# A seven-product scheme for the Fourier columns of an encoder's input projection

## The chip, the cores and the metric

The kernel runs on one core of a Trainium2 chip. The metric is device time in microseconds (us) of one execution of the whole program. A core has five engines with a queue each: TensorE (PE, matrix products, with its weight loads shown apart as PEld), VectorE (DVE), ScalarE (ACT), GpSimd (POOL) and SyncE (SP, which here only starts DMA transfers). DMA transfers are started from the queues of SP, ACT and POOL.

## What is computed

The reference is one encoder layer on 768 positions (512 of one request, 256 of another), width 2048, in float32:

```python
h = rmsnorm(x, ln_mix_g)
z = h @ w_in                       # 2048 x 2560: 1024 Fourier columns, then q 1024, k 256, v 256
of = fourier_mix(zf, w_fourier)    # Re(2-D DFT over positions and a group's 128 channels), then a 128x128 map, 8 groups
q, k = apply_rope(q), apply_rope(k)
oa = window_attention(q, k, v, attn_sink)     # 16 q heads, 4 kv heads, +-128 positions
x = x + concat(rmsnorm(of), rmsnorm(oa)) @ w_out
u = relu(rmsnorm(x, ln_mlp_g) @ w_up)
x = x + (u * u) @ w_down           # D_FF = 8192
```

and a final RMSNorm. The change is inside `z = h @ w_in`, for the Fourier columns, and in what follows it up to the attention.

## The kernel before

**Number format.** Each float32 operand of a large product is split into a high part, rounded to the multiplier's format by an ACT copy, and a low part, the DVE's difference (`split`, line 66). A product is then three matmuls: high x high, high x low, low x high. Every matmul has a 128x128 weight operand and a moving operand of up to 512 columns, and adds into one of eight PSUM banks.

**Stages.** (1) Lines 205 to 335: x is loaded in six blocks `m` of 128 rows, transposed on PE (`four`), scaled by the gains and split (`evacuate`) into `hh` and `hl`, four tiles of [128, 4, 768] each, which stay on the chip. The v columns are multiplied in the same stage (`v_proj`, line 221). The factor of the RMS norm is not applied to h: it is kept per position, and as a row `rb` (`row_scale`, line 242). (2) Lines 338 to 622: the other 2304 columns, in 36 **pieces**. A pair of 128 columns each takes four pieces, one per 512 rows of `w_in`; a piece is 512 KB of weights and 48 matmuls of 384 columns (2 column blocks x 4 k-blocks x 3 terms x 2 halves of the positions, line 602). `piece_load` and `piece_split` (lines 567, 575) fetch and split the weights, one piece ahead of the products, through two buffers `raw` and four each of `wh` and `wl`. At the end of a pair the DVE multiplies the sums by `rb` (line 615) and ACT's queue writes them to DRAM: `zf_d` (Fourier), `zk_d` (keys), `zq_d` (queries). The order of the columns is Fourier (16 pieces), k (4), q (16). (3) Attention and the output projection, interleaved. (4) The two MLP products, each already a scheme of seven products of half size.

**What runs beside the pieces.** A table `todo` (lines 540 to 560) hangs work on the middle (k + 0.5 is popped in the middle of piece k + 1) or the end of a piece. Each Fourier group has `load_group` (its z back from DRAM), `fold` (line 357, folding by symmetry on the DVE, and 4 small matmuls), `stage1` (three calls) and `stage2` (line 420, the DFT products; then ACT and DVE copy the result out, POOL squares it and adds it to `ssf`, lines 434 to 438). A group starts every second piece. `fourier_norm` (line 442) sums `ssf` with twelve one-column matmuls, one piece after the last `stage2`. Then `open_attention` loads the rotary tables, and 16 **jobs** (`keys`, `queries`, lines 485 and 495) each load half a 128-row block of k or q and its rows swapped by 32 (five DMAs, `rows2`, line 473), rotate it (one POOL and two DVE instructions, line 463), split it, and write queries back. `load_q`, `split_q` (lines 508, 529) prepare the first attention units, and `load_of` and `out_split` the first blocks of the output projection.

**What sets the order.** PE's instructions run in the order of the program text. ACT, DVE and SP do so only inside the `manual_schedule` blocks; elsewhere a scheduler at build time orders each queue. On the chip each queue runs in order: an instruction that waits holds all behind it on its engine. A tile with `bufs=n` waits until the use n allocations ago has ended.

Of the kernel before, what the change touches and what calls it, by code (L numbers as in the profile page):

```python
# [20 lines left out]
P = 128  # L21
# [4 lines left out]
NM = T // P  # L26
# [14 lines left out]
def hybrid_encoder(ctx: ExitStack, tc: tile.TileContext, a: dict):  # L41
# [74 lines left out]
    zk_d = [dpool.tile([P, T], F32, tag=f"zk{i}", name=f"zk{i}") for i in range(2)]  # L116
    zq_d = [dpool.tile([2 * P, T], F32, tag=f"zq{i}", name=f"zq{i}") for i in range(NKV)]
# [4 lines left out]
    x1_d = [[dpool.tile([P, 512], F32, tag=f"x1_{m}_{n}", name=f"x1_{m}_{n}") for n in range(4)] for m in range(NM)]  # L122

# [71 lines left out]
    with ExitStack() as ph:  # L195
        hp = ph.enter_context(tc.tile_pool(name="hp", bufs=1, reuse_waits="tile"))
        zp = ph.enter_context(tc.tile_pool(name="zp", bufs=2, reuse_waits="tile"))
        pp = ph.enter_context(tc.tile_pool(name="pp1", bufs=6, space=PSUM))
        hh, hl = [], []
        for j in range(4):  # L200
            hh.append(hp.tile([P, 4, T], F32R, tag=f"hh{j}", name=f"hh{j}"))
            hl.append(hp.tile([P, 4, T], F32R, tag=f"hl{j}", name=f"hl{j}"))
        rb = hp.tile([P, T], F32, tag="rb", name="rb")

        with tc.tile_pool(name="xp", bufs=2, reuse_waits="tile") as xp:

# [14 lines left out]
            def v_proj(m, between=None):  # L221

                pv = pp.tile([P, 512], F32, tag="ps", name="pv")
                t0 = slice(m * P, (m + 1) * P)
                high = [(hh, 0, j) for j in range(4)]
                low = [(hl, 0, j) for j in range(4)], [(hh, 1, j) for j in range(4)]
                if between is not None:
                    seq = [x for pair in zip(high, low[0]) for x in pair] + low[1]
                else:
                    seq = high + low[1] + low[0]  # L230
                for n, (l, r, j) in enumerate(seq):
                    if n == 10 and between is not None:
                        between()
                    for i in range(4):
                        nc.tensor.matmul(  # L235
                            pv[:, :256], l[j][:, i, t0], wv[j][r][:, i, :],
                            start=(n == 0 and i == 0), stop=(n == 11 and i == 3),
                        )
# [3 lines left out]
            def row_scale(m):  # L242
# [5 lines left out]
                pb = pp.tile([P, 512], F32, tag="f", name="pb", bufs=2)  # L248
# [3 lines left out]
            def load_wv(j):  # L252
                raw = xp.tile([P, 4, 256], F32, tag="raw", name="raw", bufs=4)
                nc.sync.dma_start(raw[:], w_in[:, 4 * j : 4 * j + 4, IN_W - 256 :])
                return raw
# [10 lines left out]
            def gains(r, n, c0):  # L266

                pg = pp.tile([P, 512], F32, tag="f", name="pg", bufs=2)
# [3 lines left out]
            with tc.manual_schedule(engines={mybir.EngineType.SP}):  # L272
# [3 lines left out]
                wv = [load_wv(j) for j in range(4)]  # L276
# [3 lines left out]
            def four(m):  # L280
                pts = [pp.tile([P, 512], F32, tag="ps", name="pt") for _ in range(4)]
# [6 lines left out]
            def evacuate(m, pts, js, between=lambda: None):  # L288
                ts = slice(m * P, (m + 1) * P)
                tmps = [(j, scale_rows(xp, pts[j], g0[:, 4 * j : 4 * j + 4], 4)) for j in js]  # L290
                between()
                for j, tmp in tmps:
                    nc.scalar.activation(hh[j][:, :, ts], tmp[:], AF.Copy)
                for j, tmp in tmps:
                    nc.vector.tensor_tensor(out=hl[j][:, :, ts], in0=tmp[:], in1=f32(hh[j][:, :, ts]), op=ALU.subtract)
# [4 lines left out]
            def idle(n):  # L300

                pw = pp.tile([P, 512], F32, tag="f", name="pw", bufs=2)
# [4 lines left out]
            with tc.manual_schedule(engines={mybir.EngineType.SP, mybir.EngineType.Activation, mybir.EngineType.DVE}):  # L307
# [8 lines left out]
                for m in range(NM):  # L316
# [12 lines left out]
                    if m + 3 < NM:  # L329
                        xts.append(load_x(m + 3))  # L330
                    if m > 0:
                        v_split = v_proj(m)
                v_split()
                row_scale(NM - 1)

# [4 lines left out]
        nc.sync.dma_start(cc[:], a["c_chan"])  # L340
        tabh = fp.tile([P, 4, 256], F32R, tag="tabh", name="tabh")
        tabl = fp.tile([P, 4, 256], F32R, tag="tabl", name="tabl")
        for i in range(2):
            tab = fp.tile([P, 2, 256], F32, tag="zf", name="tab", bufs=2)
            nc.sync.dma_start(tab[:], a["c_pos"][:, 2 * i : 2 * i + 2, :])
            split(tabh[:, 2 * i : 2 * i + 2, :], tabl[:, 2 * i : 2 * i + 2, :], tab[:])
        ssf = fp.tile([P, T], F32, tag="ssf", name="ssf")
        fst = {}

# [6 lines left out]

        def fold(g):

            z, wf = fst.pop(g)
            pc = pp.tile([P, 512], F32, tag="f", name="pc", bufs=2)  # L360
# [29 lines left out]
        def stage1(g, b):  # L390
            sh, sl, cw, ah, al = fst[g]
            pa = pp.tile([P, 512], F32, tag="f", name="pa", bufs=2)
# [27 lines left out]
        def stage2(g):  # L420
            ah, al = fst.pop(g)[3:]
            pe = pp.tile([P, 512], F32, tag="f", name="pe", bufs=2)
            pz = pp.tile([P, 512], F32, tag="f", name="pz2", bufs=2)
# [18 lines left out]
        def fourier_norm():  # L442
            ps_r = pp.tile([P, 512], F32, tag="f", name="ps_r", bufs=2)
# [8 lines left out]
        def open_attention():  # L452
            kp = kt["kp"] = kctx.enter_context(tc.tile_pool(name="kp", bufs=1, side="right", reuse_waits="tile"))
            for name, shape, src in (
# [4 lines left out]
                nc.sync.dma_start(kt[name][:, : src.shape[1]], src)  # L459
            kt["kdh"] = kp.tile([P, NKV, T], F32R, tag="kdh", name="kdh")  # L460
# [12 lines left out]
        def rows2(src, s):  # L473

            t0 = slice(s * HALF, (s + 1) * HALF)
            x, y = (kt["kp"].tile([P, 1, 512], F32, tag=c, name=c, bufs=n)[:, :, :HALF] for c, n in (("rx", 2), ("ry", 2)))
            z = src[:, t0].rearrange("p (o t) -> p o t", o=1)
            nc.sync.dma_start(x, z)
            for r in range(0, P, 64):
                nc.sync.dma_start(y[r : r + 32], z[r + 32 : r + 64])  # L480
                nc.sync.dma_start(y[r + 32 : r + 64], z[r : r + 32])
            rotate(x, y, t0)
            return x[:, 0, :], t0

# [1114 lines left out]
```

## Time and profile before

| what | value |
|---|---|
| time, median of 3 runs (lowest to highest) | 2608.66 us (2608.39 to 2608.85) |
| the profiled execution's own time | 2609.26 us |
| its span, first to last instruction | 2607.5 us |
| DVE, ACT, POOL busy | 67%, 41%, 9% of the span |
| DMA | 465.17 MB, mean 178 GB/s |
| granted TensorE clock | 0.999 |

A row of a group of instructions reads: line, engine, operation, output <- inputs by the program's tile names, shapes, xcount, then busy time, mean ns of one instruction, and the idle time of the engine just before them with what ended it. A row of the timeline or of the chain of waits starts with its start and its duration in us. Matmuls overlap in the pipeline, so the mean duration of one is longer than its share of PE's time. A row of the busy-time table gives a stretch of the span, its length, busy us and number of instructions of PE, PEld, DVE, ACT and POOL, the granted clock, the DMA engines' busy share and GB/s.

### The profile page before, as it was taken

How to read it: one execution, taken by the hardware profiler on the slowest of the kernel's cores; microseconds unless marked ns; L12 is line 12 of the kernel's file. 1: busy time of each engine (PE TensorE's matmuls, PEld its weight loads, DVE VectorE, ACT ScalarE, POOL GpSimd, SP SyncE). 2: the span in 40 equal slices, each digit the busy share in tenths (PEclk: the TensorE clock that was granted, in tenths of full speed). 3: DMA queues.
4: the chain of work that ended last, by engine and by line, in shares of the span. 5: the costliest groups of instructions: out<-in, count | busy, mean ns of one | idle time of the engine just before them, and what ended most of it. 6: DMA issues, size and time to landing. Idle time of an engine off the chain costs nothing.

```text
span 2607.5 us, 35144 instructions
## 1 busy us (share of the span) xinstructions
PE 2593.1 (99%) x13676; PEld 2375.5 (91%) x13676; DVE 1745.5 (67%) x2194; ACT 1079.2 (41%) x1551; POOL 247.4 (9%) x347
## 2 busy tenths in 40 slices
PE   9999999999999999999999999999999999999998
PEld 9999998888899999999999999988888888888887
DVE  6334448777655656555777787757776765777687
ACT  6233327775333333333554445433333333333335
POOL 1011212233210011000000000010000000000000
PEclk9999999999999999999999999999999999999999
DMA  5323466345664555466666666685543672554364
GB/s 178 122 95 111 137 219 187 112 126 173 198 225 151 174 169 177 147 204 244 206 213 214 224 234 213 219 325 177 182 159 111 208 249 74 177 185 157 98 209 155
DMA packets 255047, 465.17 MB, mean 178 GB/s; under 512 B 20080, under 2 KB 151712, under 8 KB 254240
## 3 DMA queue, kind: packets, MB, share of 16 engines
q1 hardware_dynamic: 189936, 305.01, 36.2%
q10 hardware_dynamic: 53120, 110.46, 11.1%
q0 software_dynamic: 11824, 47.46, 5.3%
q8 instruction: 107, 1.75, 0.3%
q14 instruction: 60, 0.49, 0.1%
HBM read 344.10 MB, written 118.75 MB: 178 GB/s over the span
## 4 chain that ended last, share of the span: by engine, by line
PE 97%; DVE 2%; DMA 1%; issue 0%; POOL 0%; ACT 0%; SPq 0%; DVEq 0%; POOLq 0%; ACTq 0%
PE pu L980 36%; PE pd L1415 35%; PE pz L602 12%; PE pm L834 9%; PE pv L235 1%; PE s L645 1%; PE o L721 1%; PE t L702 1%; PE pe L427 0%; PE pa L406 0%; PE ptx L134 0%; PE pt L134 0%; DMA raw<-in_w_in 0%; DVE p L660 0%; DVE wl L70 0%
## 5 line engine op out<-in xcount | busy, mean ns | idle before, releaser
L980 PE MATMUL pu<-xf,wh 128*128 128x384 f32 x3072 | 780.1, 334 | 0.0
L980 PEld LDWEIGHTS pu<-xf,wh 128*128 128x128 f32 x3072 | 554.0, 188 | 1.5 <-ACT o L998 1.3
L1415 PE MATMUL pd<-wh,sh 128*128 128x512 f32 x1332 | 517.7, 389 | 0.0
L1415 PE MATMUL pd<-wl,sh 128*128 128x512 f32 x1332 | 517.7, 389 | 0.0
L1415 PE MATMUL pd<-wh,sl 128*128 128x512 f32 x1332 | 517.5, 389 | 0.0
L980 PE MATMUL pu<-xf,wl 128*128 128x384 f32 x1536 | 513.1, 334 | 0.0
L1392 ACT ACTIVATE wh<-rd 128x1024 fp32r<-128x1024 f32 x200 | 202.5, 1055 | 522.0 <-PE pd L1415 424.3
L1402 DVE TENSOR_TENSOR wl<-rd,wh 128x1024 fp32r<-128x1024 f32 x200 | 236.1, 1222 | 226.1 <-ACT wh L1392 225.4
L960 ACT ACTIVATE wh<-ur 128x1024 fp32r<-128x1024 f32 x160 | 170.3, 1064 | 383.6 <-PE pu L980 207.9
L1415 PEld LDWEIGHTS pd<-wh,sl 128*128 128x128 f32 x1332 | 250.0, 188 | 52.1 <-DVE sl L1403 0.3
L1415 PEld LDWEIGHTS pd<-wh,sh 128*128 128x128 f32 x1332 | 250.1, 188 | 51.8
L1415 PEld LDWEIGHTS pd<-wl,sh 128*128 128x128 f32 x1332 | 250.1, 188 | 51.5
L980 PEld LDWEIGHTS pu<-xf,wl 128*128 128x128 f32 x1536 | 288.3, 188 | 0.0
L966 DVE TENSOR_TENSOR wl<-ur,wh 128x1024 fp32r<-128x1024 f32 x160 | 195.6, 1222 | 76.3 <-ACT wh L960 76.3
L1001 DVE TENSOR_TENSOR o<-pu,o 128x768 f32<-128x768 f32 x160 | 152.9, 956 | 121.7 <-PE pu L980 114.2
L602 PE MATMUL pz<-hh,wh 128*128 128x384 f32 x576 | 147.7, 337 | 0.0
L602 PE MATMUL pz<-hh,wl 128*128 128x384 f32 x576 | 146.2, 334 | 0.0
L602 PE MATMUL pz<-hl,wh 128*128 128x384 f32 x576 | 146.2, 334 | 0.0
L1385 DVE TENSOR_TENSOR rd<-rd 128x1024 f32<-128x1024 f32 x112 | 131.8, 1218 | 0.0
L980 PE MATMUL pu<-xs,wh 128*128 128x384 f32 x512 | 129.8, 334 | 0.0
L960 ACT ACTIVATE wh<-sx 128x1024 fp32r<-128x1024 f32 x64 | 67.9, 1063 | 130.0 <-PE pu L980 107.1
L70 DVE TENSOR_TENSOR wl<-raw,wh 128x1024 fp32r<-128x1024 f32 x56 | 68.3, 1226 | 66.5 <-ACT wh L69 64.8
(253 smaller groups left out, 3715.2 us busy)
## 6 DMA issues: line engine op xcount, KB each, us to landing
rd<-in_w_down SPq DMA_DIRECT2D x176, 512.0 KB, 4.9
ur<-in_w_up SPq DMA_DIRECT2D x128, 512.0 KB, 3.9
sr<-sd SPq DMA_DIRECT2D x95, 384.0 KB, 5.1
pd<-o ACTq DMA_DIRECT2D x60, 384.0 KB, 2.3
o<-pd POOLq DMA_DIRECT2D x60, 384.0 KB, 5.8
sd<-sm ACTq DMA_DIRECT2D x60, 384.0 KB, 2.8
raw<-in_w_in SPq DMA_DIRECT2D x40, 512.0 KB, 3.5
raw<-in_w_out SPq DMA_DIRECT2D x32, 512.0 KB, 4.2
```

What stands on the lines that cost most here:

```text
L70: nc.vector.tensor_tensor(out=lo, in0=src, in1=f32(hi), op=ALU.subtract)
L235: nc.tensor.matmul(pv[:, :256], l[j][:, i, t0], wv[j][r][:, i, :], start=(n == 0 and i == 0), stop=(n == 11 and i == 3),)
L602: nc.tensor.matmul(ps[c][s][:, :HALF], w[:, i, cs], h[j][:, i, s * HALF : (s + 1) * HALF], start=first and n == 0, stop=stop and n == 2,)
L834: nc.tensor.matmul(ps, l(k), w[:, k % 2, :], start=(k == 0 and n == 0), stop=(k == 7 and n == 2))
L960: nc.scalar.activation(wh[:], raw[:], AF.Copy)
L966: nc.vector.tensor_tensor(out=wl[:], in0=raw[:], in1=f32(wh[:]), op=ALU.subtract)
L980: nc.tensor.matmul(ps[:, t, :HALF], w[:, i, t * P : (t + 1) * P], xb[:, o, i, :], start=(s == first_of[bank] and i == 0 and n == 0), stop= ...
L1001: nc.vector.tensor_tensor(out=o, in0=src, in1=o, op=ALU.add)
L1385: add = lambda x, y, op: nc.vector.tensor_tensor(out=x[:], in0=x[:], in1=y[:], op=op)
L1392: nc.scalar.activation(wh[:], t[:], AF.Copy)
L1402: nc.vector.tensor_tensor(out=wl[:], in0=t[:], in1=f32(wh[:]), op=ALU.subtract)
L1415: nc.tensor.matmul(o, l[:, q, ts], w[:, ns], start=(j == j0 and (q, t) == (0, 0)), stop=(j == j1 and (q, t) == (1, 2)),)
```

## The change

Each group of 512 Fourier columns is cut in two halves of 256 (weight blocks `a1k`, `a2k`, k the half of the 2048 inner rows), the positions in two halves of 384 (`bk1`, `bk2`). In place of eight half-size products per group there are seven, in the order `a11, s1, s2, s3, a22, s4, a12`, where s1 = a21 + a22, s2 = s1 - a11, s3 = a11 - a21, s4 = a12 - s2, each times its own block or difference of position blocks. The sums of weights are made on the DVE from two loaded blocks; s1 and s2 are written to DRAM from POOL's queue and loaded again where a later sum needs them. The position blocks are kept unsplit (`xr`), and their differences, high and low parts are made during the products, in two buffers `xs`. A product is four pieces n (2 column groups x 2 halves of its inner rows) of 24 matmuls of 384 columns; there are 28 of them. `load7` runs 5 pieces ahead, `sum7` and `high7` 3, `low7` 2. Products share PSUM banks X, Y, Z; partial results are copied out (`out7`), added and written to `zf_d`.

The 20 pieces of k and q follow, with the split two pieces ahead and four `ps` banks in place of six; `f` banks go from two to four. `rb` is applied later: to z in `fold`, and to the rotary tables. The end-of-pair copies go from DVE to ACT. `zk_d` and `zq_d` hold 32 more rows per head, so that the swapped rows are read with one DMA, after two more writes. Fourier groups start every piece instead of every second one, `fourier_norm` stands half a piece after the last `stage2`, and jobs start every half piece. In the x stage, PSUM pools and the order of `v_proj`'s terms change.

The diff, cut to its core:

```diff
-        pp = ph.enter_context(tc.tile_pool(name="pp1", bufs=6, space=PSUM))
...
+        pp = ph.enter_context(tc.tile_pool(name="pp1", bufs=4, space=PSUM))
+        xr = [[hp.tile([P, 8, HALF], F32, tag=f"xr{k}{t}", name=f"xr{k}{t}") for t in range(2)] for k in range(2)]
+        xs = [hp.tile([P, 2, 8, HALF], F32R, tag=f"xs{i}", name=f"xs{i}") for i in range(2)]
...
+        names7 = ("a11", "s1", "s2", "s3", "a22", "s4", "a12")
+        terms7 = {"s1": ("a21", "a22", ALU.add), "s2": ("s1", "a11", ALU.subtract), "s3": ("a11", "a21", ALU.subtract), "s4": ("a12", "s2", ALU.subtract)}
+        bank7 = {"a11": "X", "s1": "Y", "s2": "X", "s3": "X", "a22": "X", "s4": "Y", "a12": "Z"}
...
+        def load7(n):
...
+            for i, x in enumerate(terms7.get(s, (s,))[:2]):
+                if n < 2 or i > 0:
+                    raw = wpool.tile([P, 4, 256], F32, tag="raw", name="raw", bufs=2)
+                else:
+                    raw = hq["p"].tile([P, 4, 256], F32, tag="wr", name="wr", bufs=5)
...
+                nc.vector.tensor_tensor(out=x[:], in0=x[:], in1=y[:], op=terms7[s][2])
+                if s in w1_d:
+                    nc.gpsimd.dma_start(w1_d[s][g][e][:], x[:])
...
+            x = xs[w % 2]
+            for i in range(4):
+                for r in range(2):
+                    for q, (l, o) in enumerate(((wh, 0), (wh, 1), (wl, 0))):
+                        nc.tensor.matmul(
+                            ps7[bank, g, r][:, :HALF], l[:, i, r * P : (r + 1) * P], x[:, o, 4 * e + i, :],
...
+        for e in range(2):
+            step(high_at, e, lambda e=e: xhigh(h1, b11, e))
+            step(low_at, e, lambda e=e: xlow(l1, b11, h1, e))
+            step(low_at, 2 + e, lambda e=e: xsum(b11, b22, b11, e))
+            step(high_at, 4 + e, lambda e=e: xhigh(h0, b11, e))
+            step(low_at, 4 + e, lambda e=e: xlow(l0, b11, h0, e))
+            step(low_at, 7 + 2 * e, lambda e=e: difference(e))
+            step(high_at, 8 + 2 * e, lambda e=e: xhigh(h1, fx["d"], e))
...
+            for n in range(NP7):
+                for fn in high_at.get(n, ()):
+                    fn()
+                sum7(n + 3)
+                high7(n + 3)
+                low7(n + 2)
+                for fn in low_at.get(n, ()):
+                    fn()
+                product7(n)
+                out7(n - 1)
+                load7(n + 5)
...
             z, wf = fst.pop(g)
+            nc.vector.tensor_tensor(out=z[:], in0=z[:], in1=rb[:], op=ALU.mult)
...
-            p0 = 5.5 + 2 * g
+            p0 = (0.5, 1.5, 2.5, 3.5, 4.5, 5.5, 6.5, 7.5)[g]
...
-        after(22.5, fourier_norm)
-        after(23, open_attention)
+        after(10, fourier_norm)
+        after(10, open_attention)
...
+            t = 10.5 + 0.5 * i
+            after(t - 0.5, lambda i=i, src=src, s=s: job_load(i, src, s))
...
-                        nc.vector.tensor_tensor(out=zs[:, hs], in0=ps[c][s][:, :HALF], in1=rb[:, hs], op=ALU.mult)
+                        nc.scalar.copy(zs[:, hs], ps[c][s][:, :HALF])
```

More of the change, by code (lines that the diff above doesn't have):

```diff
@@ L229, in v_proj @@
                 else:
-                    seq = high + low[1] + low[0]
+                    seq = [x for three in zip(high, low[1], low[0]) for x in three]
                 for n, (l, r, j) in enumerate(seq):
@@ L564, in hybrid_encoder @@
+        dst = [zk_d[i][:] for i in range(2)]
+        dst += [zq_d[i // 2][i % 2 * 2 : i % 2 * 2 + 2] for i in range(8)]
+        cols = [2048, 1024, 1280, 1536, 1792]
         n_in = 4 * len(cols)
```

307 lines of the change are left out of this document (227 added, 80 removed).

## The prediction

> **What bounds the kernel now.** I read the page first (engines, then the chain that ended last), then the busy time of the stage that changes, then the chain inside it.
>
> ```profile
> PE 2593.1 (99%) x13676; PEld 2375.5 (91%) x13676; DVE 1745.5 (67%) x2194; ACT 1079.2 (41%) x1551; POOL 247.4 (9%) x347
> PE 97%; DVE 2%; DMA 1%; issue 0%; POOL 0%; ACT 0%; SPq 0%; DVEq 0%; POOLq 0%; ACTq 0%
> 0.00:56.50 56.50, 53.14 (x425) 51.78 (x425) 38.00 (x63) 35.31 (x54) 8.47 (x22) 1.00 0.52 181
> 56.50:394.70 338.20, 338.15 (x2044) 336.50 (x2043) 150.84 (x273) 99.38 (x194) 44.45 (x33) 1.00 0.42 137
>   DVE wl L70: 0.4, 1
> ```
>
> PE carries 97% of the chain. The stage of the 36 pieces lies from 56.50 to 394.70: PE is busy 338.15 of 338.20 us there, at a granted clock of 1.00, and the last row (from the view of the products' line, its idle time) says that they ever waited once, 0.4 us. DVE is busy 45% of the stage, DMA 42%. So time leaves this stage only with PE work, and leaves it fully as long as nothing else becomes late.
>
> ```profile
> 111.59 8.32 PE pz L602 x48
> 121.01 4.22 PE pz L602 x24
> 291.43 104.11 PE pz L602 x600
> L602 PE MATMUL pz<-hh,wh 128*128 128x384 f32 x576 | 147.7, 337 | 0.0
> 29.34 5.76 PE pv L235 x48
> 1685.14 906.03 PE pd L1415 x3996
> ```
>
> The chain gives PE's real price of a matmul: 104.11 / 600 = 0.1735 us for 384 columns, not the 337 ns of the grouped row, in which neighbours overlap. A piece of 48 is 8.33 us. The three terms have 576 each: 1728 matmuls, 299.8 us. The other 38.4 us are the Fourier groups' small matmuls and the twelve of the norm; they stay.
>
> **The change, part by part.**
>
> *Matmuls.* 16 pieces x 48 = 768 go; 28 x 24 = 672 of the same shape come. The new order puts three in a row into one bank where the old one alternated. 48 matmuls of 256 columns into one bank took 5.76 us, 0.120 each; 512 columns take 906.03 / 3996 = 0.227. From 256 to 384 the step is 0.053, from 384 to 512 again 0.053: one line, with or without alternation. So 96 x 0.1735 = **16.7 us go**. The Trainium skill, "TensorE: Matmul & The Clock Gate", section Back-to-back issue gap, gives N / 2.4 + 2.5 ns for a warm isolated matmul; an estimate by it is 162.5 ns, and the saving would be 15.6 us. The trace has 173.5 for this very shape, and I use that.
>
> *DVE beside the seven products.* The time per piece on PE halves to 24 x 0.1735 = 4.16 us, and the weight work per piece doubles.
>
> ```profile
> L70 DVE TENSOR_TENSOR wl<-raw,wh 128x1024 fp32r<-128x1024 f32 x47 | 57.1, 1222 | 66.5 <-ACT wh L69 64.8 <-DMA ofr<-ofd 1.6
> L140 DVE TENSOR_TENSOR tmp<-pt,gall 128x512 f32<-128x512 f32 x24 | 15.5, 685 | 3.4 <-PE pt L134 3.4
> L615 DVE TENSOR_TENSOR zs<-pz,rb 128x384 f32<-128x384 f32 x36 | 18.5, 552 | 32.8 <-PE pz L602 32.8
> L70 DVE TENSOR_TENSOR sl<-fs,sh 128x768 fp32r<-128x768 f32 x8 | 7.6, 952 | 1.0 <-ACT sh L69 1.0
> L69 ACT ACTIVATE wh<-raw 128x1024 fp32r<-128x1024 f32 x48 | 50.6, 1060 | 81.6 <-PE pz L602 62.4 <-DMA raw<-in_w_in 6.4 <-PE s L645 4.2
> L72 ACT ACTIVATE rh<-rx 128x384 fp32r<-128x384 f32 x12 | 6.3, 525 | 48.4 <-DVE rx L471 39.0 <-DMA ql<-rl 4.9 <-DMA zq<-zs 2.8
> 11.53 4.62 DVE L70 TENSOR_TENSOR wl<-raw,wh 128x1024 fp32r<-128x1024 f32 x4
> ```
>
> 1024 columns cost 1.22 us on the DVE, 512 cost 0.69: 1.05 ns a column, so half a position block (1536 columns, not in the trace) costs an estimated 1.76. A full iteration has one weight sum, one low part and one step of positions: 1.22 + 1.22 + 1.76 = 4.20 us, against PE's 4.16. Back to back, four low parts took 4.62, 1.16 each, which makes 4.0. By `terms7` and the steps, iterations 1 to 12, bar the sixth, and 17 to 20 are full; the others are lighter. The DVE is thus level with PE; it starts about as iteration 0 of PE does, and `low7` is wanted two pieces later: 8.3 - 2.4 = 5.9 us of **margin**. 12 iterations at 4.3 lose 1.7 us of it. ACT has 1.06 + 1.49 (1536 columns by the same rule) plus copies of 0.53: 3.1 of 4.16. Cost between 0 and, at 5.0 a full iteration, 12 x 0.84 - 5.9 = 4.2; I take 0.7, near the measured durations.
>
> *Its transfers.* 44 loads of 0.524 MB replace 16; during iterations 1 to 8, two loads and one write are wanted per 4.16 us: 1.57 MB, 378 GB/s.
>
> ```profile
> 8.00:14.00 6.00, 4.95 (x40) 4.60 (x39) 5.48 (x8) 4.68 (x6) 0.00 (x0) 1.00 1.08 389
> 1690.00:1740.00 50.00, 50.00 (x221) 41.17 (x220) 25.45 (x25) 18.34 (x21) 14.51 (x27) 1.00 1.01 403
> 280.00:395.00 115.00, 115.00 (x674) 115.00 (x673) 60.83 (x89) 31.85 (x47) 23.05 (x20) 1.00 0.61 194
> DMA to landing us min/median/max: 6.6/7.6/8.7
> DMA to landing us min/median/max: 3.3/3.4/4.6
> sr<-sd SPq DMA_DIRECT2D x7, 384.0 KB, 11.6
> ```
>
> Full DMA engines moved 389 GB/s when the first weights came, and 403 with PE busy 50.00 of 50.00. So the rate is just there. The landing is dearer: a second operand has two `raw` buffers, so its load starts when the sum two pieces before is done and must land within two iterations: 8.3 less 1.2 for the sum and 0.5 to issue, 6.6 us. Landing rows (`raw`): median 3.4 us in the calm stretch 110 to 282, 7.6 in the first 16 us. Two loads and a write in flight lie between, at an estimated 1.57 MB / 389 GB/s + 1 to 2 us = 5 to 6 us. It fits; its failure is a rival below.
>
> *Start and end of the products.* Two more sums stand before the first piece; the first `wh` no longer waits for the end of `v_proj`, as its buffer is freed in the first quarter of it. A gain of up to the 0.4 us above, a loss of up to two sums, 3.5 us; I take 0. The first pieces of k are loaded long before, since the last sums end 8 pieces earlier.
>
> *Fourier groups at double pace.* What remains of the stage is 338.2 - 133.3 = 204.9 us. DVE's 150.8 loses 16 x 1.22 and 36 x 0.55 and gains 8 x 0.95 in `fold` and two more such for the tables: 121 us, 59%. ACT: 99.4 - 17 + 20 x 0.53, 93 us, 45%. Enough on average. One chain is tight: `fourier_norm` now stands 24 matmuls, 4.16 us, behind the last `stage2`.
>
> ```profile
> 281.59 0.28 PE L427 MATMUL pz<-tabh,al 128*128 128x256 f32 x1
> 281.91 0.42 DVE L432 TENSOR_SCALAR of<-pz 128x256 f32<-128x256 f32 x1 [4.11 <-PE pz L427]
> 282.47 1.47 POOL L437 TENSOR_TENSOR sq<-of 128x768 f32<-128x768 f32 x1 [17.94 <-DVE of L432]
> 284.02 1.84 POOL L438 TENSOR_TENSOR ssf<-ssf,sq 128x768 f32<-128x768 f32 x1
> 290.04 1.39 PE L445 MATMUL ps_r<-ones,ssf 128*128 128x1 f32 x12
> ```
>
> From the last product's end, 281.87, to `ssf` at 285.86 it took 3.99 us, with an idle DVE; then 4.2 us were to spare, now almost none. With one low part ahead on the DVE PE waits 1.1 us. Between 0 and 1.1, I take 0.5.
>
> *Jobs and the entry to attention.* 16 jobs stand in 8 pieces where they took 12, and bytes come closer: the 22 MB of 280 to 395 lie in some 75 to 80 us, 280 to 300 GB/s, where 194 was 0.61 of the engines (318 at 1.0).
>
> ```profile
> L469 POOL TENSOR_TENSOR ry<-ry,sinr 128x384 f32<-128x384 f32 x16 | 17.6, 1101 | 75.2 <-DMA ry<-zq 42.9 <-DMA ry<-zk 12.9 <-DMA rx<-zq 9.3
> L471 DVE TENSOR_TENSOR rx<-rx,ry 128x384 f32<-128x384 f32 x16 | 10.5, 655 | 14.5 <-POOL ry L469 10.6 <-DMA ry<-zq 3.2
> L73 DVE SCALAR_TENSOR_TENSOR rl<-rx,rh 128x384 f32<-128x384 f32 x12 | 7.7, 644 | 7.2 <-DMA ql<-rl 3.7 <-ACT rh L72 3.6
> DMA to landing us min/median/max: 2.4/3.2/8.2
> ```
>
> A job with two buffers takes issue 0.8 + landing + 1.10 + 0.66 + 0.53 + 0.64. At `rx`'s median landing of 3.2 (last row) that is 6.9 for two, 3.5 us per job, against 4.16 given. At 4.4 it is level; later jobs eat the last piece, in which `load_q` and `load_of` stand. Cost 0 to 14 (below); I take 1.0. The two extra writes per block ride in the same traffic; the reads fall from five issues to two, so SP's queue is shorter. The four `ps` banks need the end copies done within the other half's 4.16 us, and two ACT copies take 1.05: nothing, unless ACT stands 3 us behind.
>
> *Sum.* 16.7 - 0.7 - 0.5 - 1.0 = 14.5 us. The profiled execution took 2609.26 us, its span 2607.5 and 1.8 around it; it becomes 2594.8. The median shown, 2608.66, is 0.6 lower: **2594 us**.
>
> **Rivals.** *The whole 16.7.* All covers hold: 2592. It belongs to the forecast's own range, 2591 to 2598.
>
> *The DVE is the bound of the seven products.* For: 4.2 against 4.16. Against: back to back it is 4.0. At 5.0 to 5.5 a full iteration, waits between ACT and DVE included, it costs 4 to 10 us: 2596 to 2603.
>
> *Attention is entered late.* Landing at 6.6 makes a job 5.2 us: 16 take 83, and with one `load_q` behind, 87 against the 75 from the end of piece 10: 12 to 14 us of the 16.7 are given back, at 5.5 some 3. For: 85 to 95% of the DMA rate. Against: jobs can run ahead of their place, and attention needs only unit 0 at once. 2599 to 2607, say 2602. The Trainium skill, same page, section What's actually happening, holds that an idle window of about 3.4 us halves the clock until one busy window has passed. No run here shows it: the granted clock is 1.00 in every row above. An estimate by it adds 1.7 us to a wait of this kind.
>
> *Slower: the two-buffer loop.* If a second operand lands after L, an iteration takes (L + 1.7) / 2, on 16 iterations with two loads. At 8.7, the slowest of the first loads, that is 5.2: 16 x 1.04 - 5.9 = 11 us lost, still a gain. From L = 10.1 on it loses 16.7 + 5. At 11.6, which loads of 384 KB took in the full stretch 1690 to 1740, it loses 16 x 2.49 - 5.9 = 34: 2626. For it: 378 GB/s wanted of about 390. Against: there, many loads queue far ahead; here two are in flight.
>
> That fewer matmuls run than the text says cannot be: the loops fix 672.
>
> **How the numbers follow.** A change within 0.2% (5.2 us, 2603.4 to 2613.9) is about what this measurement cannot tell from none. Forecast 0.62 (faster), DVE bound 0.10 (faster), late attention 0.16 (0.10 faster, 0.06 same), two-buffer loop 0.12 (slower). Faster 0.82, same 0.06, slower 0.12. The range of 2590 to 2604 takes in the first two and most of the third.
>
> **What would show it.** Products of the seven at 24 per 4.16 us, without idle time before them; the last of them some 116.6 us after the first. If the DVE binds, PE waits for `wl` in iterations 8 to 13; if the loop does, the DVE's sums wait for DMA. The entry to attention 16 to 17 us ahead of the 394.70 at which the stage ended means that the stage kept all; `fourier_norm` waiting on POOL's `ssf` by under 1.1 us. A long wait for the first `qs` or `ofh` would be late attention. What would make it wrong: a scheduler's order on ACT or DVE that puts a group's work ahead of a split.

## The result and the profile after

The changed kernel takes **2724.11 us** (median of 4 runs, 2723.25 to 2727.26), the kernel before 2608.76 us beside it: a ratio of 1.0445, 95% interval 1.0427 to 1.0463. The change makes the kernel 115 us slower; the prediction had 14.5 us faster.

The page of the changed kernel, engines, then the slices of PE and its clock, then the chain that ended last:

```profile
PE 2588.2 (95%) x13580; PEld 2366.8 (87%) x13580; DVE 1805.1 (66%) x2230; ACT 1123.4 (41%) x1613; POOL 255.0 (9%) x359
...
PE   9999735599999999999999999999999999999998
...
PEclk9999867799999999999999999999999999999999
...
PE 89%; DMA 7%; DVE 2%; SPq 0%; issue 0%; POOL 0%; ACT 0%; DVEq 0%; POOLq 0%; ACTq 0%
```

PE executes 96 matmuls fewer, as it should, and has 97% of the chain no longer: DMA has 7% of it. Each slice is 68 us. PE's hole lies in slices 5 to 8, 272 to 545 us, and the granted clock falls in the same place. Busy time by stretch (length, then PE, PEld, DVE, ACT, POOL, then clock, DMA share, GB/s), and the chain:

```profile
56.00:180.00 124.00, 123.96 (x718) 123.64 (x717) 95.88 (x81) 57.82 (x62) 4.58 (x9) 1.00 0.82 281
180.00:300.00 120.00, 120.00 (x791) 120.00 (x790) 67.79 (x156) 54.64 (x140) 23.77 (x15) 1.00 0.38 121
300.00:420.00 120.00, 55.84 (x288) 54.03 (x287) 29.01 (x47) 19.58 (x34) 13.16 (x12) 0.72 0.28 94
420.00:520.00 100.00, 45.13 (x219) 41.41 (x218) 24.79 (x53) 18.75 (x37) 11.95 (x15) 0.71 0.35 116
```

```profile
57.23 116.41 PE p L268 x670
...
301.05 1.39 PE ps_r L651 x12
311.35 21.74 DMA ry<-zk
337.16 17.06 DMA rx<-zk
359.04 11.15 DMA rx<-zq
374.58 15.00 DMA rx<-zq
391.43 13.25 DMA rx<-zq
406.02 39.09 DMA ry<-zq x2
```

Up to 302 us the kernel does what was forecast. The seven products take 116.41 us without a wait (116.6 forecast), DMA at 281 GB/s does not hold them, and the Fourier groups keep up. At the end of `fourier_norm` nine pieces of 8.33 us are left, which would end at 377.4. Then the jobs begin, and their reads of k and q (`rx`, `ry`) take 11 to 22 us each. In the trace of before the jobs' reads (`rx`) took 3.2 at the median. The first matmul of attention (`pm`) starts at 506.97 us, where it was 395.61: 111 of the 115 us lie ahead of that line. The two stretches below lie between the issue of the keys' reads and their landing; besides these only the write of a block of queries, of the same shape, and its two small ones can be moving there. The waits from 296 to 520 us (total, times, longest) tell who passes the lateness on:

```profile
315.00:320.00 5.00, 0.02 (x1) 0.00 (x0) 0.56 (x1) 0.00 (x0) 0.00 (x0) 0.79 0.13 52
320.00:325.00 5.00, 0.00 (x0) 0.00 (x0) 0.00 (x0) 0.00 (x0) 0.00 (x0) 0.50 0.13 51
```

```profile
POOL ry L677 <- DMA ry<-zq: 132.4, 12, 30.8
DVE rx L678 <- DMA rx<-zq: 87.1, 12, 12.8
...
PEld pz L818 <- ACT zs L826: 59.3, 3, 44.2
...
PEld s L862 <- ACT qs L740: 32.9, 1, 32.9
```

Transfers wait in the queues, and yet the DMA engines are 0.13 busy and move 51 to 52 GB/s: 2 of 16 is 0.125. At 52 GB/s one read of 192 KB alone would take an estimated 3.8 us; by this estimate the rest of the 11 to 22 us is waiting behind other such transfers. POOL and DVE wait for the reads. ACT runs in order, so the copies that empty PSUM (`zs`) stand behind the jobs' copies, and PE waits for them and then for the first queries (`qs`).

**Theory A.** The new layout of k and q is `[heads, 96, T]`. A job's read is now of shape 2 x 64 x 384 and a block's large write of 2 x 64 x 768: the outermost size is 2. Such a transfer is dealt out to two of the sixteen DMA engines. **Rival B:** large reads are slow as such, or dense jobs are. **Rival C:** the dense jobs make attention late whatever the layout (the prediction's own rival). The Trainium skill, "DMA: Bandwidth & Descriptors", section "Why a DMA increments its semaphore by 16 and not by 1", states theory A as a rule: the number of engines is the largest one up to 16 that divides the outermost size, other than 1, of both access patterns. The share of 0.13 agrees with 2 of 16; I had not weighed that page against the new shapes.

### The profile page after: what moved, and what is told of

It reads as the page before. It is cut to its first block, busy times and chain, and to the rows that moved or that the text cites. A ratio compares the mean times of both kernels' runs of the same rounds, so it can differ in the third digit from the quotient of the medians.

```text
span 2722.7 us, 35114 instructions
## 1 busy us (share of the span) xinstructions
PE 2588.2 (95%) x13580; PEld 2366.8 (87%) x13580; DVE 1805.1 (66%) x2230; ACT 1123.4 (41%) x1613; POOL 255.0 (9%) x359
## 4 chain that ended last, share of the span: by engine, by line
PE 89%; DMA 7%; DVE 2%; SPq 0%; issue 0%; POOL 0%; ACT 0%; DVEq 0%; POOLq 0%; ACTq 0%
PE pu L1197 34%; PE pd L1632 33%; PE pm L1051 8%; PE p L268 4%; PE pz L818 3%; DMA rx<-zq 3%; DMA ry<-zq 2%; PE pv L391 1%; DMA ry<-zk 1%; PE s L862 1%; PE t L919 1%; PE o L938 1%; DMA rx<-zk 1%; PE pe L633 0%; PE pa L612 0%
## 5 line engine op out<-in xcount | busy, mean ns | idle before, releaser
L818 PE MATMUL pz<-xf,wh 128*128 128x384 f32 x320 | 72.5, 349 | 58.5 <-ACT zs L826 58.5
L268 PE MATMUL p<-xs,wh 128*128 128x384 f32 x448 | 113.9, 334 | 0.0
L818 PEld LDWEIGHTS pz<-xf,wh 128*128 128x128 f32 x320 | 58.8, 197 | 59.5 <-ACT zs L826 59.3
L1620 DVE TENSOR_TENSOR sl<-sr,sh 128x768 fp32r<-128x768 f32 x111 | 105.5, 950 | 0.0
```

The costliest lines, as they stand in the source:

```text
L268: nc.tensor.matmul(ps7[bank, g, r][:, :HALF], l[:, i, r * P : (r + 1) * P], x[:, o, 4 * e + i, :], start=(opens and e == 0 and i == 0 and ...
L818: nc.tensor.matmul(ps[c][s][:, :HALF], w[:, i, cs], whole[j // 2][s][o][:, 4 * (j % 2) + i, :], start=first and n == 0, stop=stop and n == 2,)
L1620: nc.vector.tensor_tensor(out=sl[:], in0=sr[:], in1=f32(sh[:]), op=ALU.subtract)
```

## The experiments

Every kernel was timed beside the kernel before, whose median was between 2608.65 and 2608.99 us; ratios are to it. Diffs are against the changed kernel unless another is named, and are cut to their core.

### Which shape costs what

**Reads by head:** each read in two, one per head.

```diff
-                nc.sync.dma_start(out, src[:, d : d + 64, t0])
+                for r in range(2):
+                    nc.sync.dma_start(out[64 * r : 64 * r + 64, 0, :], src[r, d : d + 64, t0])
```

> Only the jobs' reads are changed: each of the two reads of a job is issued as two, one per head, so that the DRAM side is 64 rows by 384 columns and no longer 2 by 64 by 384; the writes to the widened blocks stay. Theory A (a transfer whose slowest dimension has the size 2 runs on 2 of the 16 DMA engines: in the changed kernel the DMA share stands at 0.13 and 50 GB/s in whole stretches of the jobs, and 2/16 is 0.125): reads land in 3 to 5 us instead of 8 to 20, the writes of 393 KB still take some 8 us each on two engines, and the time falls from 2724 to 2594 to 2610. Rival B (the jobs stand too close, 16 in 8 pieces, and the DMA engines are simply full): the same bytes move, so 2710 to 2725. Rival C (the end-of-pair copies now stand on ACT behind the jobs' work, and four banks instead of six hold PE): the order on ACT stays, so 2700 to 2725.

Measured 2631.43 us, 1.0086 (1.0072 to 1.01). Same bytes, same place, twice the issues: 93 us of the 115 gone. Theory A's range was missed by 21 us. The writes of outermost size 2 still stand in the way: one landed after 11.37 us in this kernel's chain, and the next kernel, which undoes them too, is 20 us faster.

**Reads and writes by head:** the same, and the large write of a block in two.

```diff
-                    queue.dma_start(to[:, :64], zs[:])
+                    for r in range(2):
+                        queue.dma_start(to[r, :64], zs[64 * r : 64 * r + 64])
```

> As the kernel with reads by head, and the write of the 128 rows to a widened block is also issued as two of 64 rows, one per head. Theory A: no transfer on two engines is left; 2592 to 2600, which is what the prediction's sum gives without the slow transfers (2594), and no stretch of the jobs shows a DMA share of 0.13. Rival B: 2710 to 2725. Rival C: 2700 to 2725.

Measured 2611.33 us, 1.0011 (1.0002 to 1.002). 113 us of the loss are gone, but the 2592 to 2600 of theory A are missed. Rivals B and C, at 2700 and above, do not hold for the main loss. Something else keeps the gain; the second group of runs is about it.

**Writes by head alone.**

> Only the writes to the widened blocks are issued by head; the jobs' reads stay with a leading dimension of 2. Theory A: 16 jobs x 393 KB at 50 GB/s are 126 us of reads in one row on two engines, where 75 us of pieces are left from the end of piece 10 on; the entry to attention is some 50 to 60 us late, 2640 to 2665. Rivals B and C: 2700 to 2725.

Measured 2694.65 us, 1.033 (1.0311 to 1.0349). The loss that is left is 30 us above theory A's range, so its estimate from the bytes of the reads alone was too low. The writes alone give back 29 us, the reads alone 93, both 113. The reads carry most. That both give less than the sum can be an overlap of the two, or the limit that the second group of runs finds; no run separates these.

**The kernel before with only the new layout:** blocks of 96 rows, their three writes and a job's two reads; nothing else of the change.

> The kernel before with one part of the change alone: the key and query blocks with 96 rows per head, written with a leading dimension of 2 (and the 32 extra rows per head in two more writes), read by two transfers per job with a leading dimension of 2 instead of five. Products, copies, banks and the places of the jobs are those of before. Theory A: 16 x 393 KB of reads and 8 x 393 KB of writes on the same two engines are 190 us where the jobs have some 105; 2670 to 2710. Rival B (density) and rival C (copies on ACT, banks): their causes are not in this kernel, 2600 to 2612.

Measured 2739.18 us, 1.0501 (1.0482 to 1.052): 130 us slower, and 29 above theory A's range. So the layout needs neither the seven products nor the dense jobs to do its damage. Two stretches of this kernel show the mark again:

```profile
300.00:320.00 20.00, 20.00 (x117) 20.00 (x116) 0.56 (x1) 0.00 (x0) 1.02 (x1) 1.00 0.17 61
...
340.00:360.00 20.00, 1.50 (x7) 1.18 (x6) 8.73 (x15) 5.75 (x10) 2.04 (x2) 0.59 0.14 50
```

**Two plain copies:** each block in two arrays of 128 rows, the second with the halves of each head exchanged by four writes; a job reads 128 x 384 twice.

```diff
-            for out, d in ((x, 0), (y, 32)):
-                nc.sync.dma_start(out, src[:, d : d + 64, t0])
+            for out, d in zip((x, y), src):
+                nc.sync.dma_start(out[:, 0, :], d[:, t0])
```

> The change with the blocks kept as two plain copies (128 rows each, the second with the two halves of each head exchanged when it is written, by four writes of 32 rows on POOL's queue), so that a job still reads twice, but each read is of 128 rows. Theory A (a read whose outermost size is 2 moves on two of the sixteen DMA engines, and that alone made the change lose): the stretches with a DMA share of 0.13 are gone, a job's read lands in 3 to 5 us, and the time is near that of reads and writes by head, 2596 to 2615. Rival B (few large reads as such are slow, whatever their shape, and many small ones are fast): reads of 128 rows land in 10 us or more, and the time stays above 2640. What is left over the sum of the prediction: if it comes from the number of issues on SP's queue (four a job by head, two here), the time falls to 2594 to 2602; if from the bytes that the jobs and the blocks move (more here: each block is written twice in full), 2608 to 2615.

Measured 2613.38 us, 1.0018 (1.0009 to 1.0026). A job has again two reads of 192 KB, as in the changed kernel, and those of queries land in 4.0 and 4.4 us at the median. Rival B's large reads are out: it is the shape. Fewer issues on SP's queue did not bring the rest. The range given for the bytes holds the time; the last runs below speak against bytes as the cause.

**Outermost size 4:** the two copies as rows of 32 with a gap behind each, so that a read is 4 x 32 x 384.

```diff
+    zk_d = [[dpool.tile([4, 40, T], F32, tag=f"zk{c}{i}", name=f"zk{c}{i}") for c in "xy"] for i in range(2)]
...
+                nc.sync.dma_start(out, d[:, :32, t0])
```

> Two copies as in the run beside this one, but each block stands in rows of 32 with a gap behind them, so that a job's read has an outermost size of 4 instead of 2; its writes are of 32 rows and of no outermost small size. Theory A in its strict form (the number of engines is the outermost size where that divides 16): the share of the DMA engines in the stretches in which only the jobs read is about 0.25, the reads go at about twice the pace of after's, 100 GB/s, so that a read of 196 KB lands in 2 us of its own time and the time is 2606 to 2640. Rival B (a small outermost size is only a matter of one descriptor list being long, 2 and 4 alike slow): above 2680, share 0.13.

Measured 2649.79 us, 1.0156 (1.0138 to 1.0175): between sizes 2 and 128, as theory A has it, though 10 us above its range. The reads of queries in the chain of this kernel:

```profile
336.50 5.71 DMA rx<-zqx
345.63 7.24 DMA rx<-zqx
355.36 9.45 DMA rx<-zqx
367.22 9.66 DMA rx<-zqx
378.75 8.97 DMA rx<-zqx
389.66 8.51 DMA rx<-zqx
```

A read of 192 KB with outermost size 4 takes 5.7 to 9.7 us in the chain. With size 2 the reads of queries took 10.8 to 15 there; with 128 rows the median landing was 4.4. It was to be 2 us of transfer alone; `x` and `y` are read at once and, by theory A, through the same few engines. The share of 0.25 was not seen clean, because other transfers overlap every stretch, and a block has eight writes here, where the kernel with the plain copies has five. So the order of the doses is shown; a strict proportion, and four as the number of engines, are not.

### Where the 16.7 us went

**The layout undone:** the old blocks with one write and five reads a job; all else of the change stays.

> The change with its layout alone undone: blocks of 128 rows with one write, and five reads for a job, as before the change; the seven products and the Fourier columns' place in front stay. Theory A (the shape of the reads and writes made the whole loss): 2594 to 2612, against 2724 with the layout. Rival B (the jobs must be late anyway, since the matmuls now leave them less time): above 2640. Rival C (the 17 us over the sum that were left with reads and writes by head are the jobs packed against the attention's entry, whatever the layout): 2606 to 2614, with idle time of PE between 340 and 400 us; without C 2592 to 2598.

Measured 2608.95 us, 0.9999 (0.999 to 1.0008). The layout is the whole loss of 115 us, and without it the change is worth nothing. Rival C's waits are there. Two stretches of this kernel, PE's waits in 290 to 420 us, and the first matmuls behind the first of these waits:

```profile
340.00:360.00 20.00, 16.34 (x77) 15.93 (x77) 9.37 (x16) 5.73 (x10) 5.47 (x5) 0.83 0.77 251
...
380.00:400.00 20.00, 11.53 (x48) 9.87 (x47) 7.02 (x14) 8.91 (x17) 2.19 (x3) 0.74 0.82 255
```

```profile
PEld s L863 <- ACT qs L743: 5.0, 1, 5.0
PEld pm L1052 <- ACT ofh L69: 4.1, 1, 4.1
PEld pz L821 <- ACT zs L829: 4.0, 1, 4.0
```

```profile
348.51 1.71 PE L821 MATMUL pz<-xf,wh 128*128 128x384 f32 x4 [3.66 <-ACT zs L829]
```

PE is idle for 3.66 + 8.47 = 12.1 us in the two stretches. After the first wait it runs at half speed for a while: four matmuls take 1.71 us, where four such take 0.85 before the wait (granted clock 0.50 at 348.5 to 352 us), and the 77 matmuls of the first stretch take 16.34 us instead of 77 x 0.1735 = 13.4. The Trainium skill, "TensorE: Matmul & The Clock Gate", section "What's actually happening", says that an idle window of about 3.4 us halves the clock until a busy one has passed. This wait agrees, and a wait of 1.8 us further below left the clock at 1.00. Idle time (12.1 us), slow time in the first stretch (3.0) and the first six `pm` matmuls, which take 2.93 us where before's took 1.40, make 16.6: they take the 16.7 us up. Attention starts at 394.22 us, 1.4 ahead of before.

**The end-of-pair copies on DVE,** with reads and writes by head (2611 without).

```diff
-                        nc.scalar.copy(zs[:, hs], ps[c][s][:, :HALF])
+                        nc.vector.tensor_scalar(out=zs[:, hs], in0=ps[c][s][:, :HALF], scalar1=1.0, scalar2=None, op0=ALU.mult)
```

> Reads and writes by head (2611 before), with the copies at the end of each pair of columns on DVE instead of ACT. Rival C's part in what is left over the sum (these copies stand behind the jobs' work on ACT, and PE waits 7.3 us for them between 340 and 360 us, with the slow clock behind it): without that wait 2600 to 2606. If the jobs' packing as a whole sets the end (the last job's reads and the entry's loads): 2608 to 2614, since the wait comes back one step later. DVE has the sums of the jobs too, so a loss to 2615 to 2625 is possible if the copies now wait behind those.

Measured 2616.82 us, 1.0029 (1.0017 to 1.004): slower, in the range given for copies that wait behind the jobs' sums, and above that of the jobs' packing. PE waits 4.8 us at the copies' banks in place of 7.3, and 13.0 us for the first queries in place of 3.0. The lateness moves to the next line.

So the jobs as a whole came under suspicion (**theory R**): they can start only when the Fourier groups have freed their space, and then 16 of them need their own time. For the first half, the waits of SP's queue in 290 to 320 us with the layout undone: the loads of the rotary tables (L665), which stand ahead of the jobs' reads, wait for the norm's last matmuls.

```profile
SPq L665 <- PE ps_r L651: 10.2, 1, 10.2
```

For the second half, two groups of rows of the view by tile, of before and of the layout undone, give the first and last start of the jobs' first and last DVE instruction (the 17th `rx` belongs to attention):

```profile
L470 DVE TENSOR_TENSOR rx<-rx,cosr x17: 550/559/1287, 297.6 to 408.4; 128x384 f32<-128x384 f32 x16, 64x512 f32<-64x512 f32 x1
...
L73 DVE SCALAR_TENSOR_TENSOR rl<-rx,rh x12: 551/559/1395, 322.1 to 387.5; 128x384 f32<-128x384 f32 x12
```

```profile
L678 DVE TENSOR_TENSOR rx<-rx,cosr x17: 551/558/1301, 309.8 to 409.4; 128x384 f32<-128x384 f32 x16, 64x512 f32<-64x512 f32 x1
...
L73 DVE SCALAR_TENSOR_TENSOR rl<-rx,rh x12: 551/558/1372, 334.8 to 386.3; 128x384 f32<-128x384 f32 x12
```

The jobs start 12.2 us later than before and end 1.2 earlier: 76.5 us for 16, 4.8 each. PE alone would be done at 377.4.

**Fourier groups 0.75 of a piece apart,** layout undone, to start the jobs earlier. Two more kernels do it with the scaling of a group's rows on POOL, and by one piece instead of one and a half.

```diff
-            p0 = (0.5, 1.5, 2.5, 3.5, 4.5, 5.5, 6.5, 7.5)[g]
+            p0 = (0.5, 1.5, 2.0, 3.0, 3.5, 4.5, 5.0, 6.0)[g]
...
-        after(10, fourier_norm)
-        after(10, open_attention)
+        after(8.5, fourier_norm)
+        after(8.5, open_attention)
...
-            t = 10.5 + 0.5 * i
+            t = 9 + 0.5 * i + 0.5 * (i // 4)
```

> The change with its layout undone (2609 before), and the Fourier groups 0.75 of a piece apart instead of one piece, so that the norm stands at piece 8.5 instead of 10 and the jobs from 9 on instead of 10.5, with half a piece of air after every fourth. Theory R (the 17 us that the seven products save are given back because the 16 jobs can start only when the Fourier groups' buffers are free, 12 us later than before the change in microseconds, and then need 4.8 us each, so that the entry to attention stays at 394 us): the first job's rotation comes at 297 to 299 us instead of 309.8, the entry at 378 to 383, the time is 2592 to 2600. Rival S (the DMA engines, 0.74 to 0.82 full between 340 and 400 us, are the bound by their bytes, wherever the jobs stand): 2604 to 2610. What may spoil it: the groups take an estimated 6.0 us of DVE each and the pieces' low parts 0.92 in each 6.25 us, so that DVE is more than full and PE may wait in 180 to 250 us; then 2598 to 2606.

> The same with the multiplication of each group's rows by the norm's factors (0.96 us on DVE) on POOL, so that DVE has 5.0 + 0.9 us of 6.25. Theory R: 2591 to 2598, without a wait of PE between 180 and 250 us. Rival S: 2604 to 2610.

> A smaller dose: the norm at piece 9, the jobs from 9.5 on, one piece (8.3 us) earlier than with the layout undone alone. Theory R: about two thirds of the gain of the run with 1.5 pieces, the entry at 384 to 387 us, 2597 to 2603. Rival S: 2604 to 2610.

Measured 2617.52 us, 1.0036 (1.0022 to 1.0049); with POOL 2623.3, 1.0053 (1.0041 to 1.0066); one piece 2614.93, 1.0023 (1.0014 to 1.0032). All three miss. A stretch of the first of them, and PE's waits in its Fourier groups and its entry:

```profile
240.00:300.00 60.00, 52.12 (x314) 51.42 (x315) 29.70 (x67) 24.37 (x63) 14.48 (x8) 0.89 0.25 86
```

```profile
PEld pa L601 <- ACT sh L69: 7.2, 3, 3.0
PEld pa L602 <- DVE sl L70: 5.0, 3, 3.1
PEld pz L821 <- ACT zs L829: 4.1, 2, 3.9
PEld pm L1052 <- ACT ofh L69: 1.8, 1, 1.8
```

At the entry PE waits only 1.8 us, as theory R has it, but it waits 12 us in the groups, with slow matmuls behind (clock 0.89): with these buffers a group's chain from `fold` to `stage1` could not be pressed below a piece, though DVE is busy only half of the stretch. That speaks for length in series rather than load; with the scaling on POOL PE's wait for `sh` grows to 12.4 us. So in the first of the three the norm's matmuls came at 306.8 us instead of 301.6, the first rotation later, not earlier (315.9), and attention started at 403 us.

**Jobs one piece later,** layout undone: `t = 11.5 + 0.5 * i`.

> The change with its layout undone, and the jobs from piece 11.5 on instead of 10.5 (8.3 us later). Theory R: the entry moves from 394 to 399 to 403 us and the time to 2614 to 2619. Rival T: no change, 2607 to 2611.

Measured 2609.75 us, 1.0001 (0.9992 to 1.0011): theory R's range is missed, and that of rival T, in which something at the entry holds PE, is met. The first rotation stays at 309.8 us and the last `rl` moves from 386.3 to 394.8, yet attention starts at 394.45: it does not wait for the last job. What stands at the entry is the first queries' load, which kept its place and has two jobs fewer ahead of it. In this kernel's chain that load is issued at 385.49 us, and PE waits 10.1 us for it. That the two cancel is argued, not shown. It names a second thing to move.

**Twelve jobs,** layout undone: the third group's queries are rotated unit by unit in attention, as the fourth's were. And **the kernel before with twelve jobs,** for the price of that edit.

```diff
-            if g < NKV - 1:
+            if g < NKV - 2:
...
-        jobs += [(queries, (g, i), zq_d[g][2 * i : 2 * i + 2], s) for g in range(NKV - 1) for i in range(2) for s in range(2)]
+        jobs += [(queries, (g, i), zq_d[g][i * P : (i + 1) * P, :], s) for g in range(NKV - 2) for i in range(2) for s in range(2)]
```

> The change with its layout undone (2609 before), and 12 jobs instead of 16: the third group's queries are rotated unit by unit in attention, as the fourth's are. Theory R (the stage is held to its old length by the Fourier groups and then 16 jobs of 4.8 us in a row): 4 jobs fewer free 19 us, so PE's own work sets the entry: first unit's matmul at 377 to 381 us instead of 394.2, no wait of PE for the zs copies, and the time is 2592 to 2596 plus the price of rotating six more units in attention, which the run beside it gives. Rival S (DMA bytes): each job moves 0.8 MB, so it gains too, but only some 8 us. Rival T (PE is held up by something else at the entry, such as the first loads from queries' and Fourier rows): the entry stays at 392 to 395 us.

> The kernel before with 12 jobs instead of 16. Its products end at 394.7 us with PE never waiting, so no theory gives it a gain at the entry: 2607 to 2609 if the six more units' rotations are hidden in attention, 2610 to 2622 if they are not. The difference of the two kernels with 12 jobs is then what the seven products are worth when the jobs do not hold them back: 14 to 17 us by theory R, under 8 by S, under 3 by T.

Measured 2603.55 us, 0.998 (0.9971 to 0.9988), against 2613.34, 1.0018 (1.0009 to 1.0027). The edit alone costs the kernel before 4.6 us; with it on both sides the change is worth 9.8 us. That is less than the 14 to 17 of theory R and more than the 8 of the bytes (rival S), and the wait for the copies that theory R took for gone is still there. Attention now starts right behind the products, by this kernel's chain:

```profile
347.59 36.35 PE pz L821 x192
385.76 1.65 PE pm L1052 x6
```

The products end at 383.94 instead of 377; the one wait for `zs` at 345 us (3.7 us, and the slow clock behind it) was to account for that; the next runs take it away.

**Free banks:** the fourth pair of columns uses the four PSUM banks that the Fourier groups have left, so that it waits for no copy. With 12 jobs, with 16, and with 16 and the first queries' and Fourier rows' loads ahead of the last jobs.

```diff
-                ps = [[pp.tile([P, 512], F32, tag="ps", bufs=4, name="pz") for _ in range(2)] for _ in range(2)]
+                ps = [[pp.tile([P, 512], F32, tag="f" if pair == 3 else "ps", bufs=4, name="pz") for _ in range(2)] for _ in range(2)]
```

> 12 jobs, layout undone, and the fourth pair of columns in the four PSUM banks that the Fourier groups no longer use, so that its first matmuls wait for no copy. Theory R (the end copies behind the jobs on ACT cost 3.7 us of waiting and about 2.2 of half clock, 5.9 in all): products end at 378 us instead of 383.9, and the time is 2597 to 2599. If the wait comes back as a wait for weights or at the entry: 2601 to 2604.

> The same banks with all 16 jobs (layout undone; 2609 without the banks). Theory R: the products end at 378 us, but the first queries' loads stand behind the jobs, so that the entry stays at 391 to 395 us with a longer wait of PE at it, and the time is 2605 to 2610. If the wait for the copies was all that held the gain back: 2600 to 2603.

> As the run beside it, with the loads of the first two units' queries and of the Fourier rows ahead of the last jobs (the last job then runs inside attention, whose third unit is the first that needs it). Theory R: the entry follows the products at 380 to 385 us, and the time is 2593 to 2600. If the jobs' reads and writes hold the first loads back by bytes: 2603 to 2610. If the third unit waits for the last job: a new wait of PE at 395 to 410 us, and a gain of under 5 us.

With 12 jobs **2597.76 us, 0.9957 (0.9944 to 0.9969)**, the fastest of all and ahead of both kernels; with 16 jobs 2608.13, 0.9998 (0.9989 to 1.0007); with the early loads 2605.59, 0.9988 (0.9979 to 0.9997), above theory R's range and in the one given for the bytes. The chain, a stretch and a wait of the first:

```profile
301.94 74.99 PE pz L821 x432
378.75 1.65 PE pm L1052 x6
```

```profile
360.00:380.00 20.00, 18.41 (x105) 18.00 (x104) 6.44 (x9) 8.19 (x13) 2.18 (x3) 1.00 0.84 245
```

```profile
PEld pm L1052 <- ACT ofh L69: 1.8, 1, 1.8
```

432 matmuls in 74.99 us, no wait, the end at 376.93, half a microsecond ahead of the 377.4 worked out above. Attention starts 16.9 us ahead of before's 395.61 and 16.0 ahead of the 394.76 of before with the same edit, and the kernel is 15.6 us ahead of that one. DMA is 0.84 busy in the last stretch and holds nothing back. The kernels with 16 jobs stay below that share between 340 and 400 us (0.82 at most with the layout undone, 0.78 with the early loads), so the bytes were not the bound. The same banks with 16 jobs give nothing, by this kernel's longest wait and the longest with the early loads:

```profile
PEld s L863 <- ACT qs L743: 10.9, 1, 10.9
```

```profile
PEld pm L1052 <- ACT ofh L69: 10.2, 1, 10.2
```

The time that the banks gave is lost again at the entry, where 3.0 us more go to `ofh`. With the early loads the wait is for `ofh` alone, the Fourier rows, which are loaded into the jobs' `ry` buffers. Of the edits tried only the two together brought the gain: fewer jobs, and no wait for the copies.

## Why the prediction was wrong, by its own steps

- *Matmuls, 16.7 us.* Right. The seven products took 116.41 us for 670 recorded matmuls, 0.1737 each, and with the way free attention starts 16.0 us earlier than in the kernel before with the same twelve jobs.
- *DVE 0.7, transfers, start 0.* Right in substance; PE waited once in 56 to 174 us, 0.4 us for the first `wl`, and never for the DVE after that, so the 0.7 was too much. The rival of the two-buffer loop, the only one on the slower side, did not appear: 281 GB/s were moved there.
- *`fourier_norm` 0.5.* It cost 0.2 us, by PE's wait for `ssf`: `ps_r` follows the last matmuls of its piece in the chain at 301.05 us.
- *"The two extra writes per block ride in the same traffic; the reads fall from five issues to two, so SP's queue is shorter."* **This step failed, and with it the sign.** I counted issues and bytes, and took "rx's median landing of 3.2 (last row)" over to reads of another shape. That row was of 128 x 384; the new reads are 2 x 64 x 384 and took 10.8 to 22 us in the chain, at a DMA share of two engines. Undoing the shapes takes away 115.2 us of the time; putting them alone into the kernel before adds 130. No term of the sum stood for this; the nearest rival, late attention, reckoned with landings of at most 6.6.
- *"Cost 0 to 14 (below); I take 1.0"* for the jobs and the entry, with 3.5 us a job. With the old layout this term measured about 16, by 4.8 us a job. My loop of a job held its own instructions and one landing. The chain of the kernel with the layout undone shows what I left out, the queries' writes back to DRAM, for whose landing their two buffers wait:

```profile
375.68 4.38 DMA qh<-rh
380.69 4.92 DMA qh<-rh
387.49 5.45 DMA rx<-ql
```

- *The rival "attention is entered late"* was the mechanism, with 0.16. It had 12 to 14 us given back of 16.7, and "jobs can run ahead of their place" against it. They can, but not ahead of the Fourier groups' space: the first rotation came at 309.8 us in two kernels whose places differ by a piece, and in both SP's queue waits 10.2 us for the norm's last matmuls before it loads the tables. The DMA share that spoke for it (0.85 to 0.95 there) was not what decided: at 0.84 nothing waited.
- *The clock.* The prediction said that no run showed the halving. Here the clock is 0.50 in the stretch without a matmul, and 1.71 us for four matmuls stand behind the wait of 3.66.

What stays open: where the last 1.1 us of 16.7 go with 12 jobs (0.7 of them are missing when attention starts, and PE waits 1.8 us there for `ofh`), why the reads and the writes together give less than their sum, and how much of the remaining 10.9 us at the entry of the 16-job kernel belongs to the writes' landing and how much to the order on ACT.

## What to carry to other kernels

Before a landing time is taken from a row, compare the shapes of the access patterns, not only the bytes and the issues: an outermost size of 2 turned a read of 3 us into one of 11 and more, and a low DMA share beside engines that wait for DMA was its mark. When a bound engine gets shorter work, measure the longest chain beside it that does not shrink; here Fourier groups and 16 jobs in series filled PE's old time to within 1.4 us, and the gain came only when that chain was shortened and a wait for banks taken out. A chain's length is not the load of its engines, so a busy share of a half did not tell here whether it could be pressed.

## What the runs showed of the hardware

- Transfers of outermost size 2, waiting in the queues with hardly anything else, kept the sixteen DMA engines 0.13 busy and moved 51 to 52 GB/s; for two engines that is an estimated 26 GB/s each. Undoing the shape of the reads gave 93 us, of the writes 29, of both 113.
- PE's clock was granted at 0.50 in a stretch without matmuls. After a wait of 3.66 us the next four matmuls took 1.71 us instead of 0.85; a wait of 1.8 us left the clock at 1.00.
